# Moving the modulation dots of a decoder block's output stage, and the order of channels in its first two w_out tiles

## The chip, the core and the metric

The kernel runs on one core of one Trainium2 chip. The metric is the device time of one execution in microseconds (us). The engines are TensorE (PE; PEld is its loading of stationary weights), VectorE (DVE), ScalarE (ACT), GpSimd (POOL) and SyncE (SP), which here only issues transfers between HBM and the on-chip memory.

## The reference

One decoder block over 512 tokens and 1024 channels, in fp32. Cut to what matters:

```python
mod = c @ w_ada + b_ada                      # 6 x 1024 numbers
sh_a, sc_a, gt_a, sh_m, sc_m, gt_m = split(mod, 6)
h = modulate(rmsnorm(x, g_mix), sh_a, sc_a)
z = h @ w_in                                 # q, k, v, latents and two gates zga, zgb
o_nsa = nsa_attention(...)                   # 8 heads
o_mla = mla_attention(...)                   # 8 heads
y = sigmoid(zga) * (o_nsa @ w_o_nsa) + sigmoid(zgb) * (o_mla @ w_o_mla)
x = x + gt_a * (y @ w_out)
h = modulate(rmsnorm(x, g_mlp), sh_m, sc_m)
x = x + gt_m * (square(relu(h @ w_fc1)) @ w_fc2)
return rmsnorm(x, g_final)
```

The modulation `c @ w_ada` is 48 columns of 128 results. sh_a and sc_a are wanted first; gt_a, sh_m, sc_m and gt_m (the late ones) only behind the attention.

## The kernel before, in words

Channels lie on the 128 partitions, the 512 tokens on the free axis. 1024 channels are 8 tiles. Every product of an fp32 weight with an fp32 activation is made of three matmuls of rounded (fp32r) parts: each is split into a high part (a copy on ACT, L183 for weights, L192 for activations) and a low part (a subtraction on DVE, L184 and L193), and `mm3` (L197, L198, L199) multiplies high by high, high by low and low by high. A unit of weights is 128x1024 fp32, 512 KB. `wsplit` loads it on SP's queue into one of **four** `w_raw` buffers (L175) and splits it into w_hi and w_lo (three buffers each); with `far` the parts are called wp_hi and wp_lo and lie in another pool.

A modulation dot (`ada_dot`, L105 and L107) is not a matmul. It loads a 128x1024 piece of w_ada, also 512 KB, on SP's queue into one of the same four w_raw buffers, and DVE multiplies it by c and sums over the free axis into one column of `mod`. `ada_late(u)` makes two dots and adds the bias (L118); `ada_fill(end)` calls it for the next units up to `end`. Units 8 to 23 are the late ones, 32 dots in all.

The stages around the change, with their times in the profiled execution:

- MLA heads (about 232 to 328 us). The order is a string by hand, `ORDER`: `p` prepares the V products (vm), `a` makes q and k of a pair of heads, `b` their scores and softmax, `m` their values, `g1` one of the sixteen late gates (`gate_unit`: 24 matmuls with a w_z unit, then a tanh into tab), and `e1` one unit of the late modulation. `e1` stands there twice (units 8 and 9).
- Late gates (about 328 to 380): `fill(16)` makes what is left of the sixteen gates, and `ada_fill(12)` units 10 and 11.
- Output projections (about 380 to 421): for each of 8 tiles n, o_nsa by one half of w_o into the accumulator ps_acc and o_mla by the other half into ps_s. DVE multiplies each by its gate (ya, L759; yb, L761), POOL adds them into yb (L762), ACT and DVE split the sum into y*n*h and y*n*l. Behind each tile `ada_fill(12 + n + 1)` asks for one unit (12 to 19).
- w_out (from about 421): four whole tiles and then four in halves of the tokens, each a sum over all eight y tiles, 24 matmuls with 512 columns for a whole tile. Units 20 to 23 are asked for behind them. Then the MLP.

Nearly all of this is one stream for a scheduler. It writes a static order of instructions for each engine, in the order of the code as far as data and buffers allow, with the splits of weights ahead of others (`high_priority`). On the chip each engine, and SP's queue of transfers, then runs its list strictly in that order. A transfer into a w_raw buffer is issued once the last reader of that buffer is done. PSUM has two buffers for ps_acc and two for ps_s.

Of the kernel before, what the change touches and what calls it, by code (L numbers as in the profile page):

```python
# [13 lines left out]
ALU = mybir.AluOpType  # L14
PSUM = bass.MemoryType.PSUM

P = 128
S = 512
D = 1024
KT = D // P  # L20
# [19 lines left out]
FAR = 2  # L40
EV = "v"
NA = ["1"]
ORDER = "f0 t0 s0 t1 f1 h v0 c s1 v1 s2 g1 v2 g1 q w0 s3 w2 v3 w1 k g1 p g1 g1 a1 w3 a0 b1 a2 e1 b0 a3 m1 b3 e1 m3 m0 g1 b2 m2"


@with_exitstack
def block_kernel(ctx: ExitStack, tc: tile.TileContext, d):
    nc = tc.nc
# [3 lines left out]
    def psum(tag):  # L52
        bufs = PB[tag]
        return ps.tile([P, S], F32, name="ps_" + tag, tag=tag, bufs=bufs)
# [11 lines left out]
    def tmp(name):  # L66
        return sb.tile([P, S], F32, name=name, tag="tmp", bufs=NB["tmp"])

    def f(ap):
        return ap.bitcast(F32)  # L70


    def wtile(shape=(P, 1024)):
        return sb.tile(list(shape), F32, name="w_raw", tag="w_raw", bufs=NB["raw"])
# [97 lines left out]
    def wsplit(src, shape, far=False):  # L172
        n = int(np.prod(shape))
        raw = wtile()
        nc.sync.dma_start(raw[:, :n], src)  # L175
        if far:
            hi = sb.tile([P, 1280], F32R, name="wp_hi", tag="p", bufs=NB["p"])
            lo = sb.tile([P, 1280], F32R, name="wp_lo", tag="p", bufs=NB["p"])
        else:
            hi = sb.tile([P, 1024], F32R, name="w_hi", tag="w_hi", bufs=NB["hi"])  # L180
            lo = sb.tile([P, 1024], F32R, name="w_lo", tag="w_lo", bufs=NB["lo"])
        with tc.high_priority():
            nc.scalar.activation(hi[:, :n], raw[:, :n], AF.Copy)  # L183
            nc.vector.tensor_tensor(lo[:, :n], raw[:, :n], f(hi[:, :n]), op=ALU.subtract)  # L184
        pat = "p (a b) -> p a b" if len(shape) == 2 else "p (a b c) -> p a b c"
        kw = dict(zip("abc", shape))
        return hi[:, :n].rearrange(pat, **kw), lo[:, :n].rearrange(pat, **kw)

    def split(name, src, get):
        hi = get(name + "h", F32R)  # L190
        lo = get(name + "l", F32R)
        nc.scalar.activation(hi, src, AF.Copy)  # L192
        nc.vector.tensor_tensor(lo, src, f(hi), op=ALU.subtract)  # L193
        return hi, lo

    def mm3(out, w, x, first, last):
        nc.tensor.matmul(out, w[0], x[0], start=first, stop=False)  # L197
        nc.tensor.matmul(out, w[0], x[1], start=False, stop=False)  # L198
        nc.tensor.matmul(out, w[1], x[0], start=False, stop=last)  # L199

    def dense(out, unit, rhs, tok=ALL):
        hi, lo = unit
        n = len(rhs)
        for k in range(n):
            mm3(out[:, tok], (hi[:, k], lo[:, k]), (rhs[k][0][:, tok], rhs[k][1][:, tok]), k == 0, k == n - 1)
# [25 lines left out]
    h = []  # L231
# [192 lines left out]
    w2 = w2_th[:, 0:256].rearrange("p (k n c) -> p k n c", k=2, n=2)  # L424
# [240 lines left out]
    def gate_unit(i):  # L665
        pz = z_unit(9 + i)
        t = big_n(f"tab{i}")
        nc.scalar.activation(t, pz, AF.Tanh, scale=0.5)
        tab[i] = t
# [3 lines left out]
    def ada_late(u):  # L673
        for r in range(2):
            ada_dot(2 * u + r)
        bias_col(2 * u, 2)
# [5 lines left out]
    gi = [0]  # L682

    def fill(n):
        for _ in range(n):
            if gi[0] < 16:
                gate_unit(gi[0])
                gi[0] += 1

    ai = [8]  # L690

    def ada_fill(end):

        while ai[0] < min(end, 24):
            ada_late(ai[0])
            ai[0] += 1

    mqk, msc, lat = {}, {}, {}
    for step in ORDER.split():
        op, a = step[0], int(step[1:] or 0)  # L700
# [27 lines left out]
            fill(a)  # L728
        elif op == "e":
            ada_fill(ai[0] + a)  # L730
    fill(16)
    ada_fill(12)


    oh = []
# [15 lines left out]
    y = []  # L751
    for n in range(KT):
        w = wsplit(d["w_o"][n], (KT, P))
        pa = psum("acc")
        dense(pa, (w[0][:, 0:4], w[1][:, 0:4]), o_sp[0:4])
        pb = psum("s")
        dense(pb, (w[0][:, 4:8], w[1][:, 4:8]), o_sp[4:8])
        ta = tmp("ya")
        nc.vector.scalar_tensor_tensor(ta, tab[n], 1.0, pa, op0=ALU.add, op1=ALU.mult)  # L759
        tb = tmp("yb")  # L760
        nc.vector.scalar_tensor_tensor(tb, tab[8 + n], 1.0, pb, op0=ALU.add, op1=ALU.mult)  # L761
        nc.gpsimd.tensor_tensor(tb, ta, tb, op=ALU.add)  # L762
        y.append(split(f"y{n}", tb, big_a))
        ada_fill(12 + n + 1)
    st1 = Stats(KT, -1)

    def out_tile(n, pa, tok):
        nc.vector.scalar_tensor_tensor(xt[n][:, tok], pa[:, tok], modb[:, GTA + n:GTA + n + 1], xt[n][:, tok],
                                       op0=ALU.mult, op1=ALU.add)
        st1.add(xt[n], tok=tok)  # L770

    for n in range(KT - NH1):
        w = wsplit(d["w_out"][n], (KT, P))
        pa = psum("acc")
        dense(pa, w, y)
        out_tile(n, pa, ALL)

    for k in range(KT):
# [2 lines left out]
    ws = [wsplit(d["w_out"][n], (KT, P), n < KT - 2) for n in range(KT - NH1, KT)]  # L781
    for hf, tok in enumerate(HALVES):
        for n, w in zip(range(KT - NH1, KT), ws):
            pa = psum("acc")
# [170 lines left out]
    for qq in range(4):  # L955
# [3 lines left out]
        if qq == 0:  # L959
            ws = [wsplit(d["w_fc1"][UNITS[n]], (KT, P), n < FAR) for n in range(NPRE)]  # L960
# [6 lines left out]
        for i, n in enumerate(UNITS):  # L967
# [3 lines left out]
            if i in pre:  # L971
                pa = pre[i]
            else:
                w = wsplit(d["w_fc1"][8 * qq + n], (KT, P))
                pa = psum(("acc", "acc", "m", "o")[i % 4])
# [4 lines left out]
        if qq < 3:  # L980
            for i in range(2):
                w = wsplit(d["w_fc1"][8 * qq + 8 + UNITS[i]], (KT, P))
                pa = psum("acc")
# [14 lines left out]
    ws = [wsplit(d["w_fc2"][3, n], (KT, P), n < KT - 2) for n in range(nf, KT)]  # L998
    for hf, tok in enumerate(HALVES):
        for n, w in zip(range(nf, KT), ws):  # L1000
            pa = psum("s")
# [5 lines left out]
        k = 0  # L1007
# [120 lines left out]
```

## Time and profile before

| | us |
|---|---|
| median of three runs | 830.43 (828.70 to 832.08) |
| the profiled execution, its own time | 831.55 |
| its span, from the first to the last record | 829.8 |
| PE busy in the span | 798.3 (96%) |
| DVE busy | 606.2 (73%) |
| ACT busy | 392.1 (47%) |
| POOL busy | 148.0 (18%) |

The profile is of one execution. An engine's busy time counts its instructions, without the waits; a busy PE may still run at the lower of its two clocks, 1.2 instead of 2.4 GHz, which the granted clock (PEclk, as a share of full speed) shows. A wait in the trace is the idle time ahead of an instruction, put down to the one that released it last. Since each engine runs in a fixed order, an idle PE means that the next matmul on its list lacks an operand or a place to write to; whether that costs time is seen from the starts of the matmuls around it.

### The profile page before, as it was taken

Reading aid. Unit: us, or ns where it says so; the run is one execution under the profiler, and the core shown is the slowest. Engines: PE = TensorE matmul, PEld = TensorE weight load, DVE = VectorE, ACT = ScalarE, POOL = GpSimd, SP = SyncE. Lnnn points to the kernel's source line nnn. Section 1 sums busy time; section 2 is a strip of 40 time slices with the busy share of each in tenths; the row PEclk is TensorE's granted clock in tenths of the full one; section 3 lists DMA queues with packets and bytes.
Section 4 is the critical chain, followed back from the end, with each engine's and each line's share of the span. In section 5 each row is a group of like instructions: output and inputs, shape, how many; then the busy total and the mean of one; then the engine's idle time right before and its main releaser. Section 6 shows DMA issues by size and latency. Waiting matters only on the chain.

```text
span 829.8 us, 11895 instructions
## 1 busy us (share of the span) xinstructions
PE 798.3 (96%) x4444; PEld 646.3 (78%) x4444; DVE 606.2 (73%) x1177; ACT 392.1 (47%) x742; POOL 148.0 (18%) x125
## 2 busy tenths in 40 slices
PE   5899999999999999999989999999999999999896
PEld 3687668665577665888768998899889988998895
DVE  5988758887657886367877648887668766877854
ACT  4358526475333443222232437644564456445741
POOL 1500000000000000002330003460336033613200
PEclk8999999999999999999999999999999999999998
DMA  9683161010032122587647302233323332332303
GB/s 336 233 275 139 56 224 51 27 51 26 26 128 76 52 77 69 170 260 255 228 159 254 110 18 85 94 103 127 101 77 103 127 102 76 103 128 77 102 1 102
DMA packets 31004, 99.76 MB, mean 120 GB/s; under 512 B 3521, under 2 KB 5761, under 8 KB 30946
## 3 DMA queue, kind: packets, MB, share of 16 engines
q1 hardware_dynamic: 30880, 98.89, 36.0%
q8 instruction: 35, 0.57, 0.3%
q14 instruction: 23, 0.19, 0.1%
q0 software_dynamic: 64, 0.11, 0.1%
q10 hardware_dynamic: 2, 0.00, 0.0%
HBM read 96.89 MB, written 2.10 MB: 119 GB/s over the span
## 4 chain that ended last, share of the span: by engine, by line
PE 74%; DVE 11%; DMA 5%; ACT 3%; POOL 3%; issue 3%; SPq 0%; DVEq 0%; POOLq 0%; ACTq 0%
PE ps_acc L197 10%; PE ps_acc L199 10%; PE ps_acc L198 10%; PE ps_s L858 8%; PE ps_t L858 6%; PE ps_t L391 4%; DVE junk L107 3%; PE ps_o L572 3%; DMA w_raw<-in_w_ada_dram 3%; PE ps_s L644 2%; PE ps_o L657 2%; PE ps_s L197 1%; PE ps_s L198 1%; PE ps_s L199 1%; POOL yb L762 1%
## 5 line engine op out<-in xcount | busy, mean ns | idle before, releaser
L184 DVE TENSOR_TENSOR w_lo<-w_raw,w_hi 128x1024 fp32r<-128x1024 f32 x76 | 96.1, 1266 | 62.8 <-ACT w_hi L183 62.4
L183 ACT ACTIVATE w_hi<-w_raw 128x1024 fp32r<-128x1024 f32 x76 | 80.2, 1058 | 125.5 <-PE ps_acc L198 68.8
L346 ACT ACTIVATE p<-p,nm 128x128 f32<-128x128 f32 (+3 forms) x96 | 53.3, 556 | 58.1 <-DVE nm L344 56.8
L198 PE MATMUL ps_acc<-hl,w_hi 128*128 128x512 f32 x200 | 80.1, 400 | 0.0
L199 PE MATMUL ps_acc<-hh,w_lo 128*128 128x512 f32 x200 | 80.0, 400 | 0.0
L197 PE MATMUL ps_acc<-hh,w_hi 128*128 128x512 f32 x200 | 79.3, 397 | 0.0
L379 DVE COPY pT<-ps_t 128x512 f32<-128x512 f32 (+1 forms) x72 | 42.4, 598 | 31.1 <-PE ps_o L572 16.6
L816 ACT ACTIVATE ws_hi<-wsum 128x512 fp32r<-128x512 f32 x56 | 35.3, 631 | 58.0 <-POOL wsum L829 55.3
L107 DVE SCALAR_TENSOR_TENSOR junk<-w_raw,cb 128x1024 bf16<-128x1024 f32 x32 | 40.0, 1255 | 16.8 <-DMA w_raw<-in_w_ada_dram 16.7
L829 POOL TENSOR_TENSOR wsum<-w_raw 128x512 f32<-128x512 f32 x28 | 39.5, 1410 | 64.9 <-DMA w_raw<-in_w_fc_dram 53.4
L829 POOL TENSOR_TENSOR wsum<-wsum,w_raw 128x512 f32<-128x512 f32 x28 | 45.9, 1640 | 25.6 <-DVE ws_lo L817 25.2
L817 DVE TENSOR_TENSOR ws_lo<-wsum,ws_hi 128x512 fp32r<-128x512 f32 x56 | 42.9, 796 | 4.9 <-ACT ws_hi L816 2.5
L198 PEld LDWEIGHTS ps_acc<-hl,w_hi 128*128 128x128 f32 x200 | 37.6, 188 | 11.0 <-issue 4.3
L199 PEld LDWEIGHTS ps_acc<-hh,w_lo 128*128 128x128 f32 x200 | 37.6, 188 | 10.0 <-issue 3.1
L197 PEld LDWEIGHTS ps_acc<-hh,w_hi 128*128 128x128 f32 x200 | 37.6, 188 | 9.8 <-issue 3.0
L197 PE MATMUL ps_acc<-h2h,w_hi 128*128 128x512 f32 x112 | 43.6, 389 | 0.0
L198 PE MATMUL ps_acc<-h2l,w_hi 128*128 128x512 f32 x112 | 43.6, 389 | 0.0
L199 PE MATMUL ps_acc<-h2h,w_lo 128*128 128x512 f32 x112 | 43.6, 389 | 0.0
L762 POOL TENSOR_TENSOR yb<-ya,yb 128x512 f32<-128x512 f32 x8 | 17.5, 2185 | 133.3 <-DVE yb L761 123.2
L858 PE MATMUL ps_t<-t,ws_hi 128*128 128x256 f32 x224 | 40.5, 281 | 0.7 <-DVE t L946 0.4
L391 PEld LDWEIGHTS ps_t<-ident,p 128*128 128x128 f32 x240 | 27.7, 141 | 16.3 <-issue 6.3
L817 DVE TENSOR_TENSOR w_lo<-w_raw,w_hi 128x1024 fp32r<-128x1024 f32 (+1 forms) x28 | 31.0, 1107 | 10.2 <-ACT w_hi L816 10.2
(478 smaller groups left out, 2305.1 us busy)
## 6 DMA issues: line engine op xcount, KB each, us to landing
w_raw<-in_w_fc_dram SPq DMA_DIRECT2D x64, 512.0 KB, 3.3
w_raw<-in_w_ada_dram SPq DMA_DIRECT2D x32, 512.0 KB, 3.9
w_raw<-in_w_z_dram SPq DMA_DIRECT2D x25, 512.0 KB, 3.6
w_ada<-in_w_ada_dram SPq DMA_DIRECT2D x16, 512.0 KB, 6.6
w_raw<-in_w_c_dram SPq DMA_DIRECT2D x8, 512.0 KB, 4.5
w_raw<-in_w_o_dram SPq DMA_DIRECT2D x8, 512.0 KB, 4.4
w_raw<-in_w_out_dram SPq DMA_DIRECT2D x8, 512.0 KB, 3.3
w_raw<-in_w_g_dram SPq DMA_DIRECT2D x8, 448.0 KB, 7.2
```

Of the source, the lines that this page charges most:

```text
L107: nc.vector.scalar_tensor_tensor(junk, w, 1.0, cb, op0=ALU.mult, op1=ALU.mult, accum_out=mod[:, col:col + 1])
L183: nc.scalar.activation(hi[:, :n], raw[:, :n], AF.Copy)
L184: nc.vector.tensor_tensor(lo[:, :n], raw[:, :n], f(hi[:, :n]), op=ALU.subtract)
L197: nc.tensor.matmul(out, w[0], x[0], start=first, stop=False)
L198: nc.tensor.matmul(out, w[0], x[1], start=False, stop=False)
L199: nc.tensor.matmul(out, w[1], x[0], start=False, stop=last)
L346: nc.scalar.activation(o, o, AF.Exp, bias=nm, scale=-1.0, accum_out=sm)
L379: nc.vector.tensor_copy(dst, src)
L391: nc.tensor.transpose(pp[:, off:off + P], aps[i][:, kb * P:(kb + 1) * P], ident)
L817: nc.vector.tensor_tensor(lo, src, f(hi), op=ALU.subtract)
L829: nc.gpsimd.tensor_tensor(t, sums[x_] if isinstance(x_, int) else x_, y_, op=ALU.add)
L858: nc.tensor.matmul(out, w[a_][:, k], x[k][b_], start=(first and k == 0 and j == 0), stop=(k == 3 and j == 2), skip_group_check=True)
```

## The change

The sixteen late units are asked for at other places, one of the adds changes its engine, and two tiles of w_out are made together.

- `ORDER` has `e1` four times: units 8 to 11 are made in the MLA heads, one ahead of two gates near `p`, two at the old places, one ahead of the last pair's scores.
- Behind every second late gate one unit is asked for (12 to 17). Units 18 and 19 follow the projections of tiles 1 and 3; behind the other projections there is none. Units 20 to 23 stay.
- For the projections of tiles 6 and 7 the sum of ya and yb is made on DVE, for the other six still on POOL.
- The first two w_out tiles are summed side by side, the first in ps_acc and the second in ps_s: channels 0 to 5 of the first, 0 to 5 of the second, then 6 and 7 of the first and 6 and 7 of the second.

```diff
-ORDER = "... k g1 p g1 g1 a1 w3 a0 b1 a2 e1 b0 a3 m1 b3 e1 m3 m0 g1 b2 m2"
+ORDER = "... k g1 p e1 g1 g1 a1 w3 a0 b1 a2 e1 b0 a3 m1 b3 e1 m3 m0 g1 e1 b2 m2"
...
-    fill(16)
-    ada_fill(12)
+    while gi[0] < 16:
+        fill(1)
+        if gi[0] % 2 == 0:
+            ada_fill(min(ai[0] + 1, 18))
+    ada_fill(18)
...
-        nc.gpsimd.tensor_tensor(tb, ta, tb, op=ALU.add)
+        (nc.vector if n >= KT - 2 else nc.gpsimd).tensor_tensor(tb, ta, tb, op=ALU.add)
         y.append(split(f"y{n}", tb, big_a))
-        ada_fill(12 + n + 1)
+        if n in (1, 3):
+            ada_fill(ai[0] + 1)
...
+    NL = 2
+    ws = [wsplit(d["w_out"][n], (KT, P)) for n in range(2)]
+    pas = [psum("acc"), psum("s")]
+    for ks in (range(KT - NL), range(KT - NL, KT)):
+        for w, pa in zip(ws, pas):
+            for k in ks:
+                mm3(pa, (w[0][:, k], w[1][:, k]), y[k], k == 0, k == KT - 1)
     for n in range(KT - NH1):
-        w = wsplit(d["w_out"][n], (KT, P))
-        pa = psum("acc")
-        dense(pa, w, y)
+        if n < 2:
+            pa = pas[n]
+        else:
+            w = wsplit(d["w_out"][n], (KT, P))
+            pa = psum("acc")
+            dense(pa, w, y)
         out_tile(n, pa, ALL)
```

On SP's queue, from the V products to the late gates, the order before was this (w_uv holds the V weights, w_uqk the q and k weights, w_z the gates' weights, w_ada the dots'; the first two w_z loads here are those of gates 3 and 4, the next ones of gate 5 on):

```order
L175 DMA w_raw<-in_w_uv_dram 128x1024
L175 DMA w_raw<-in_w_z_dram 128x1024 x2
L175 DMA w_raw<-in_w_uqk_dram 128x1024 x3
L105 DMA w_raw<-in_w_ada_dram 128x1024 x2
L175 DMA w_raw<-in_w_uqk_dram 128x1024
L105 DMA w_raw<-in_w_ada_dram 128x1024 x2
L175 DMA w_raw<-in_w_z_dram 128x1024 x8
```

With the change it is this:

```order
L175 DMA w_raw<-in_w_uv_dram 128x1024
L105 DMA w_raw<-in_w_ada_dram 128x1024 x2
L175 DMA w_raw<-in_w_z_dram 128x1024 x2
L175 DMA w_raw<-in_w_uqk_dram 128x1024 x3
L105 DMA w_raw<-in_w_ada_dram 128x1024 x2
L175 DMA w_raw<-in_w_uqk_dram 128x1024
L105 DMA w_raw<-in_w_ada_dram 128x1024 x2
L175 DMA w_raw<-in_w_z_dram 128x1024
L105 DMA w_raw<-in_w_ada_dram 128x1024 x2
L175 DMA w_raw<-in_w_z_dram 128x1024 x2
L105 DMA w_raw<-in_w_ada_dram 128x1024 x2
```

The loads of pairs of dots now stand ahead of those of the gates, and between them: behind the load of gate 5 two of dots, then gates 6 and 7, two of dots, gates 8 and 9. On DVE in the MLA heads, at the end of the third pair's scores (L344 and L369 are of the softmax, L379 copies transposed p for PE, L360 is the softmax's reciprocal), the order before was:

```order
L107 SCALAR_TENSOR_TENSOR junk,mod<-w_raw,cb 128x1024
L360 RECIPROCAL rc<-sm 128x4
L107 SCALAR_TENSOR_TENSOR junk,mod<-w_raw,cb 128x1024
L369 TENSOR_SCALAR p<-p,rc 128x128
L369 TENSOR_SCALAR p<-p,rc 128x384
L369 TENSOR_SCALAR p<-p,rc 128x512
L118 TENSOR_TENSOR modb<-mod,cols 128x2
L379 COPY pT<-ps_t 128x512 x2
L184 TENSOR_TENSOR w_lo<-w_raw,w_hi 128x1024
L379 COPY pT<-ps_t 128x256
L379 COPY pT<-ps_t 128x512
```

With the change:

```order
L107 SCALAR_TENSOR_TENSOR junk,mod<-w_raw,cb 128x1024
L360 RECIPROCAL rc<-sm 128x4
L107 SCALAR_TENSOR_TENSOR junk,mod<-w_raw,cb 128x1024
L369 TENSOR_SCALAR p<-p,rc 128x128
L369 TENSOR_SCALAR p<-p,rc 128x384
L369 TENSOR_SCALAR p<-p,rc 128x512
L118 TENSOR_TENSOR modb<-mod,cols 128x2
L379 COPY pT<-ps_t 128x512 x2
L379 COPY pT<-ps_t 128x256
L184 TENSOR_TENSOR w_lo<-w_raw,w_hi 128x1024
L379 COPY pT<-ps_t 128x512
L184 TENSOR_TENSOR w_lo<-w_raw,w_hi 128x1024
```

Two splits of gate weights stand among the copies now, in place of one. On DVE in the projections, around tile 4 (one tile of the eight), the order before was:

```order
L193 TENSOR_TENSOR y3l<-yb,y3h 128x512
L107 SCALAR_TENSOR_TENSOR junk,mod<-w_raw,cb 128x1024
L759 SCALAR_TENSOR_TENSOR ya<-tab_2172,ps_acc 128x512
L107 SCALAR_TENSOR_TENSOR junk,mod<-w_raw,cb 128x1024
L761 SCALAR_TENSOR_TENSOR yb<-tab_3018,ps_s 128x512
L118 TENSOR_TENSOR modb<-mod,cols 128x2
L184 TENSOR_TENSOR w_lo<-w_raw,w_hi 128x1024
L114 SCALAR_TENSOR_TENSOR amlp<-mod,badd,cols 128x1
L193 TENSOR_TENSOR y4l<-yb,y4h 128x512
```

With the change (ya and yb stand on lines 763 and 765 there):

```order
L193 TENSOR_TENSOR y3l<-yb,y3h 128x512
L763 SCALAR_TENSOR_TENSOR ya<-tab_2181,ps_acc 128x512
L765 SCALAR_TENSOR_TENSOR yb<-tab_3063,ps_s 128x512
L184 TENSOR_TENSOR w_lo<-w_raw,w_hi 128x1024
L193 TENSOR_TENSOR y4l<-yb,y4h 128x512
```

The dots and their sums of columns are gone from between the products. On PE in the first w_out tile the order before was:

```order
L199 MATMUL ps_acc<-y5h,w_lo 128x512
L197 MATMUL ps_acc<-y6h,w_hi 128x512
L198 MATMUL ps_acc<-y6l,w_hi 128x512
L199 MATMUL ps_acc<-y6h,w_lo 128x512
L197 MATMUL ps_acc<-y7h,w_hi 128x512
L198 MATMUL ps_acc<-y7l,w_hi 128x512
L199 MATMUL ps_acc<-y7h,w_lo 128x512
L197 MATMUL ps_acc<-y0h,w_hi 128x512
```

With the change, from the last product of y5 with the second tile on:

```order
L199 MATMUL ps_s<-y5h,w_lo 128x512
L197 MATMUL ps_acc<-y6h,w_hi 128x512
L198 MATMUL ps_acc<-y6l,w_hi 128x512
L199 MATMUL ps_acc<-y6h,w_lo 128x512
L197 MATMUL ps_acc<-y7h,w_hi 128x512
L198 MATMUL ps_acc<-y7l,w_hi 128x512
L199 MATMUL ps_acc<-y7h,w_lo 128x512
L197 MATMUL ps_s<-y6h,w_hi 128x512
```

The products with y6 and y7 stand behind 36 others now, where y6 stood behind 18 and y7 behind 21.

## Rows read from the trace of the kernel before

**Rows 1.** The page: busy time, share of the span and instructions of each engine.

```profile
PE 798.3 (96%) x4444; PEld 646.3 (78%) x4444; DVE 606.2 (73%) x1177; ACT 392.1 (47%) x742; POOL 148.0 (18%) x125
```

**Rows 2.** Table by stage: stretch, length, engines' busy us (instructions), PEclk, DMA share, GB/s.

```profile
core 0: us, PE busy (x) PEld busy (x) DVE busy (x) ACT busy (x) POOL busy (x), PEclk, DMA share, GB/s
232.00:281.00 49.00, 48.95 (x208) 36.87 (x207) 34.89 (x81) 19.38 (x45) 2.45 (x4) 1.00 0.30 97
281.00:328.00 47.00, 46.64 (x224) 26.71 (x223) 36.22 (x90) 19.39 (x49) 0.00 (x0) 1.00 0.18 55
328.00:380.00 52.00, 52.00 (x230) 42.99 (x229) 26.78 (x43) 14.42 (x19) 0.00 (x0) 1.00 0.70 229
380.00:421.00 41.00, 39.74 (x171) 31.74 (x170) 32.91 (x55) 11.46 (x14) 13.48 (x7) 1.00 0.66 212
421.00:433.00 12.00, 8.45 (x30) 6.37 (x29) 10.68 (x11) 5.25 (x7) 4.00 (x2) 0.86 0.53 175
```

**Rows 3.** PE's waits: engine, operation, line, released by: us, times, longest.

```profile
PE ps_acc L197 <- ACT y7h L192: 3.0, 1, 3.0
...
PE ps_acc L197 <- DVE ya L759: 1.0, 1, 1.0
```

**Rows 4.** Timeline of PE, projections: start, us, line, operation [idle before <- releaser].

```profile
407.71 0.39 PE L199 MATMUL ps_s<-ohl,w_lo 128*128 128x512 f32 x1
409.08 0.47 PE L197 MATMUL ps_acc<-ohl,w_hi 128*128 128x512 f32 x1 [0.97 <-DVE ya L759]
...
414.48 0.40 PE L199 MATMUL ps_s<-ohl,w_lo 128*128 128x512 f32 x1
415.17 0.47 PE L197 MATMUL ps_acc<-ohl,w_hi 128*128 128x512 f32 x1 [0.29 <-DVE amlp L114]
```

**Rows 5.** Timeline of DVE, projections: one modulation dot.

```profile
407.10 1.22 DVE L107 SCALAR_TENSOR_TENSOR junk<-w_raw,cb 128x1024 bf16<-128x1024 f32 x1
```

**Rows 6.** Timeline of PE, first w_out tile.

```profile
420.79 0.39 PE L197 MATMUL ps_acc<-y0h,w_hi 128*128 128x512 f32 x1
...
425.35 0.39 PE L199 MATMUL ps_acc<-y6h,w_lo 128*128 128x512 f32 x1
428.76 0.51 PE L197 MATMUL ps_acc<-y7h,w_hi 128*128 128x512 f32 x1 [3.03 <-ACT y7h L192]
429.79 0.80 PE L198 MATMUL ps_acc<-y7l,w_hi 128*128 128x512 f32 x1 [0.52 <-DVE y7l L193]
...
432.89 0.39 PE L199 MATMUL ps_acc<-y1h,w_lo 128*128 128x512 f32 x1
```

**Rows 7.** Timeline of DVE and POOL, first w_out tile.

```profile
423.92 0.68 DVE L193 TENSOR_TENSOR y6l<-yb,y6h 128x512 fp32r<-128x512 f32 x1
425.12 0.67 DVE L761 SCALAR_TENSOR_TENSOR yb<-tab,ps_s 128x512 f32<-128x512 f32 x1
425.96 2.09 POOL L762 TENSOR_TENSOR yb<-ya,yb 128x512 f32<-128x512 f32 x1 [3.05 <-DVE yb L761]
426.85 2.28 DVE L184 TENSOR_TENSOR wp_lo<-w_raw,wp_hi 128x1024 fp32r<-128x1024 f32 x1
```

**Rows 8.** Timeline of DVE and PE at the V products in the MLA heads.

```profile
232.62 0.69 DVE L525 TENSOR_TENSOR o<-o,ps_m 128x512 f32<-128x512 f32 x1 [0.31 <-PE ps_m L523]
234.21 0.69 DVE L379 COPY vm<-ps_acc 128x512 f32<-128x512 f32 x1 [0.90 <-PE ps_acc L199]
235.37 0.39 PE L197 MATMUL ps_acc<-w_hi,ckv0h 128*128 128x512 f32 x1
```

**Rows 9.** Timeline of DVE and ACT, third pair of MLA heads.

```profile
294.56 1.20 DVE L107 SCALAR_TENSOR_TENSOR junk<-w_raw,cb 128x1024 bf16<-128x1024 f32 x1
296.81 1.06 ACT L183 ACTIVATE w_hi<-w_raw 128x1024 fp32r<-128x1024 f32 x1 [1.61 <-PE ps_acc L198]
297.90 1.23 DVE L184 TENSOR_TENSOR w_lo<-w_raw,w_hi 128x1024 fp32r<-128x1024 f32 x1
```

**Rows 10.** The page's DMA issues (KB each, us to landing), then a wait of DVE.

```profile
w_raw<-in_w_z_dram SPq DMA_DIRECT2D x25, 512.0 KB, 3.6
w_ada<-in_w_ada_dram SPq DMA_DIRECT2D x16, 512.0 KB, 6.6
...
DVE junk L107 <- DMA w_raw<-in_w_ada_dram: 16.7, 11, 3.6
```

More of the change, by code (lines that the diff above doesn't have):

```diff
@@ L42 @@
 NA = ["1"]
-ORDER = "f0 t0 s0 t1 f1 h v0 c s1 v1 s2 g1 v2 g1 q w0 s3 w2 v3 w1 k g1 p g1 g1 a1 w3 a0 b1 a2 e1 b0 a3 m1 b3 e1 m3 m0 g1 b2 m2"
+ORDER = "f0 t0 s0 t1 f1 h v0 c s1 v1 s2 g1 v2 g1 q w0 s3 w2 v3 w1 k g1 p e1 g1 g1 a1 w3 a0 b1 a2 e1 b0 a3 m1 b3 e1 m3 m0 g1 e1 b2 m2"
 @with_exitstack
```

## The prediction

> **What bounds the kernel now.** The page comes first: PE is busy for 798.3 us, 96% of the span [rows 1]. The matmuls of both kernels are the same, so time can only come out of stretches in which PE stands still or runs at a lower clock, and it can only be lost by making new ones. The table by stage shows where such stretches lie in the part that the change touches [rows 2]. The MLA heads (232 to 328) leave PE idle for 0.05 and 0.36 us, the late gates (328 to 380) for nothing; there 230 matmuls take 52.00 us, 0.226 us each, and I take 0.23 as the step from one matmul to the next. The output projections (380 to 421) lose 1.26 us, and the first w_out tile (421 to 433) 3.55 us, at a granted clock of 0.86 where every other stretch has 1.00. The list of PE's waits names the causes there: y7h with 3.0 us, ya with 1.0 [rows 3].
>
> **What the change takes away.** Two losses, each measured from start to start, less the normal steps.
>
> First, the projections. The matmul at 407.71 is followed by one at 409.08, 1.37 us later in place of 0.23, and the one at 414.48 by one at 415.17, 0.69 us later [rows 4]. The first waits for ya, which must empty the accumulator; on DVE a modulation dot of 1.22 us, begun at 407.10, stands just before ya [rows 5]. Together 1.14 + 0.46 = 1.6 us. In the changed order no dot stands on DVE between the first ya and the last, and the column products (amlp) that stood there too are done in the gates. I take all 1.6 us as gained.
>
> Second, y7. The last y6 matmul starts at 425.35, the first y7 one at 428.76, the next at 429.79, and the normal step is back at 432.89 [rows 6]. That is nine steps in 7.54 us; nine normal ones are 2.07, so 5.47 us are lost. The first two steps are 3.18 and 0.80 us too long; the other 1.49 us go to the lower of the two clocks, 1.2 GHz, which PE was granted right after standing still (the 0.86 of that stretch). Without the standing still I expect no fall of the clock: with the stop of 0.97 us at 409.08 in it, the stretch of the projections was granted 1.00 [rows 2, 4].
>
> Is y7 in time now? The chain is yb (425.12, 0.67 us), the add on POOL (2.09), y7h on ACT, y7l on DVE [rows 7]. w_out starts at 420.79 [rows 6]. Before, PE asks for y7h after 21 matmuls; now after 39, at 420.79 + 39 x 0.23 = 429.8, and for y7l at 430.0. Suppose DVE is as late as before: yb ends at 425.8, the add on DVE takes as long as yb (0.68, my estimate from the yb row, the same size), so y7h can start at 426.5 and is ready near 427.2. Behind the add stand w_lo and wp_lo; wp_lo took 2.28 us beside POOL's add, and 1.23 is what a subtraction of this size took without it [rows 9], so y7l ends near 426.5 + 1.23 + 1.23 + 0.68 = 429.6. That is 0.4 us before it is wanted, with DVE as late as it was; and it will be less late, because twelve of the sixteen dots that lay in the projections' code are gone from it. y6 is wanted at 429.1 and was split by 424.6. w_out[1] is now wanted after 18 matmuls instead of 24, 1.4 us sooner, and its split is on DVE before y6's. So the wait goes and nothing takes its place there. Gain so far: 1.6 + 5.5 = **7.1 us**.
>
> **What it adds and moves.** The dots keep their number and their price (1.22 us [rows 5] and a short read of the sum, about 1.3 together). They move to DVE's queue in the MLA heads and the gates, and their 512 KB loads on SP's queue go in front of the late gates' weights, in the same four w_raw buffers. In the gates PE needs one tile of weights in 5.5 us (24 x 0.23); DVE has 26.78 of 52 us busy, ACT 14.42 and the DMA engines 70% [rows 2], so two dots for every second gate are hidden there: cost nothing. If that cover were gone, the eight dots that come to the gates would cost up to 1.3 us each. Three transfers of x now stand on SP's queue before two gate loads, which are wanted some 10 us later: nothing.
>
> In the MLA heads DVE is the busy engine (34.89 of 49 and 36.22 of 47 us [rows 2]) and PE's next work often comes out of it, so moved work costs there. Three places:
> - The V products. Two dots, 2.6 us, now stand between the first and the second copy of vm. Before, DVE was idle for 0.90 us ahead of the second copy, at 234.21, and ahead of that it had added o (128x512 as the copy, so about 0.7), which now stands later [rows 8]. So the second copy comes 2.6 - 0.9 - 0.7 = 1.0 us later, at 235.2, and ends at 235.9. The fourth product, begun at 235.37, writes over that copy's buffer: 0.5 us late. I take 0.4, between 0 and the 1.3 of one dot.
> - Gate weights 6 and 7. Before, these were loaded long ahead. Now two dots of the next unit hold two of the four buffers, so each load is issued only when a dot has been done; in the old trace the second of two begins at 294.56 [rows 9] and is done at 295.8. A w_z load lands after 3.6 us [rows 10], ACT's split takes 1.06, so the second subtraction could start at about 295.8 + 3.6 + 1.06 = 300.5. DVE would reach it at 297.90 + 0.42 + 1.23 + 0.69 = 300.2 (the subtraction's old start, a short copy, one subtraction, a copy). DVE waits some 0.3 us, does one subtraction more than before (1.23), and the copies of the transposed p that PE wants stand behind it. PE has 18 gate matmuls in that place, 4.1 us, for cover. I take 0.7; from 0 (fully covered) to 3.7, if a load takes the 6.6 us that is the median of the w_ada loads at the start [rows 10].
> - Gate weights 8 and 9, the same with the last pair of heads: dots after om0's copy, the subtractions among the copies of the last pair. I take 0.8; 0 to 3.8.
>
> Below nothing: PE's order changes between the two kinds of matmul 17 times here instead of 19, worth at most 0.2 us. Sum of the additions **1.9 us**, from -0.2 to 8.8.
>
> All else is the same: behind the second w_out half the order is unchanged on every engine. Eight dots remain for the w_out tiles in both. Without the stop in front of y7, DVE has 5.5 us less for them, some four dots, and the six w_out tiles that follow take PE far longer than the eight (8 x 1.3 = 10.4 us): hidden, nothing.
>
> **Sum.** 7.1 - 1.9 = 5.2 us less. The profiled execution took 831.55 us (span 829.8 and 1.75 around it), so 826.3 on its scale; the median of the runs is 830.43, 1.1 us less than the profiled one, and against it the forecast is **825.2 us**.
>
> **The rivals.**
> - *The heads give most of it back.* Loads of 4 to 5 us in place of 3.6 at both places of gate weights, each held on DVE and passed on to PE, make the additions 3 to 7 us: 826.5 to 830.5, middle 828.4. For it: DVE's queue is in order, and the two loads of a pair overlap. Against: filler matmuls stand beside each. The Trainium skill has a rule that speaks for this rival: *DMA: Bandwidth & Descriptors*, section Rules for kernel authors, says to issue a DMA early, compute, and wait for it late, so that the fixed cost is hidden; the change does the opposite for four gate loads. No row here shows a late w_z load, since none was late. Chance 0.22.
> - *y7 is late all the same.* The margin above is 0.4 us if DVE is as late as before, and wp_lo waits for a w_out load. If w_out[5] lands 3 us late, y7l is late by 2.6: 827.8. For it: SP's queue sends the eight w_out loads one after the other, and DVE's order has wp_lo ahead of y6l and y7l. Against: these loads now follow w_o loads with few dots between. Chance 0.08.
> - *Slower.* The four buffers starve the heads: at gate weights 6, 7, 8 and 9 DVE stands still for a whole load of 3.6 us, because every load must wait for a dot, every dot for its own load, in one queue; PE's fillers (gates 5 to 7) need the very weights that are late and are no cover. 4 x 3.6 = 14.4 us in place of the 1.5 that I have: 825.2 + 12.9 = 838 us. It decides as soon as such waits take 5.2 us more than I have, since the gain is gone then. Against: in the old trace DVE waited 11 times for a w_ada load, 16.7 us in all and 3.6 at most [rows 10], and PE stood still for none of it. Chance 0.05.
> - *It does not do what it says*: the scheduler might have put the dots back. The order shows that it has not. Chance nil.
>
> **How the numbers follow.** Forecast, additions of 0 to 3 us: chance 0.65, 823.3 to 826.3. Faster by over 0.5% (about what a measurement of this kernel can tell from no change) means below 826.3: the forecast's 0.65 and a little of the first rival, 0.66. Within 0.5%, 826.3 to 834.6: most of the first rival and the second, 0.29. Slower: 0.05. The range takes in the forecast, the late y7 and most of the first rival: **822.3 to 829.6**, where the lower end also allows 1 us for the scatter of the runs.
>
> **What would show it.** In the changed profile: no wait of PE for y7h or y7l, and a clock of 1.00 between 400 and 440; no wait for ya over 0.3 us. The loss in the heads should show as PE idle time of 1 to 3 us between 232 and 330, with DVE's w_lo waiting for w_hi and that for a w_z load. PE idle of 5 us or more there, or a wait for y7l, would make the forecast wrong.

## The result, and the profile after

The changed kernel takes 822.03 us (median of 6 runs, 820.9 to 823.5); the kernel before took 830.59 us beside it (6 runs, 828.7 to 832.4). The ratio is 0.9896, with an interval of 0.9880 to 0.9912: 8.6 us less, of which 7.3 to 10.0 are sure. The forecast was 825.2 us, 5.2 us less, with a range down to 822.3. The time lies just below that range: the direction was right, the size was not. Medians and ratios are of undisturbed executions; one execution of the order string alone, below, took 1579.85 us and is left out.

The profiled execution of the changed kernel took 820.9 us, with a span of 819.1. Its page (the row of busy times, answering to [rows 1]):

```profile
PE 796.0 (97%) x4444; PEld 645.2 (79%) x4444; DVE 608.7 (74%) x1179; ACT 393.0 (48%) x742; POOL 141.1 (17%) x123
```

The table by stage of the changed kernel, with the columns of [rows 2]; the stretches are the same stages, moved to where they now lie:

```profile
229.40:278.40 49.00, 48.95 (x209) 36.64 (x207) 36.15 (x85) 17.96 (x43) 2.45 (x4) 1.00 0.33 108
278.40:325.00 46.60, 46.60 (x223) 27.12 (x221) 37.48 (x92) 20.62 (x48) 0.00 (x0) 1.00 0.27 85
325.00:377.00 52.00, 52.00 (x231) 42.53 (x231) 35.73 (x66) 15.29 (x20) 0.00 (x0) 1.00 0.83 279
377.00:416.00 39.00, 39.00 (x170) 31.70 (x170) 27.16 (x30) 12.69 (x15) 10.95 (x6) 1.00 0.36 121
416.00:427.00 11.00, 11.00 (x51) 9.06 (x50) 6.50 (x9) 3.89 (x5) 0.00 (x0) 1.00 0.49 150
```

PE is busy for the whole length of every stretch but the first, which lacks 0.05 us, and the clock is 1.00 in all five. The 1.26 us that the projections lost, the 3.55 us and the clock of 0.86 at the first w_out tile, and the 0.36 us in the second half of the heads are gone. No wait of PE for ya, y7h, y7l or pT is left in its list of waits.

To compare many executions I use one table from here on. It gives, from the starts of matmuls in each trace, the length of four stages: **heads** (first V product to first projection, so with the late gates), **projections** (to the first w_out matmul), **w_out** (to the MLP's first matmul into ps_s, three behind its very first) and **MLP** (to the end of the span), all in us. By this count the projections of the kernel before begin at 374.70 us, earlier than the rounded 380 of the list of stages.

| kernel | first V product at | heads | projections | w_out | MLP |
|---|---|---|---|---|---|
| before | 228.84 | 145.86 | 46.09 | 52.22 | 356.77 |
| after | 226.22 | 145.53 | 44.33 | 46.79 | 356.26 |
| gain | 2.62 | 0.33 | 1.76 | 5.43 | 0.51 |

The gains add up to 10.65 us, the difference of the two spans. The three stages that the change touches give **7.52 us**. The 2.62 us ahead of them belong to no edit: the list of work is the same there, and the eleven executions of other kernels below reach the first V product between 226.83 and 228.52 us, whatever their edits. That is the scatter of one execution, and medians are less open to it.

### The profile page after: what moved, and what is told of

The parts are those of the page before. It is cut to its first block, busy times and chain, and to the rows that moved or that the text cites. A ratio compares the mean times of both kernels' runs of the same rounds, so it can differ in the third digit from the quotient of the medians.

```text
span 819.1 us, 11898 instructions
## 1 busy us (share of the span) xinstructions
PE 796.0 (97%) x4444; PEld 645.2 (79%) x4444; DVE 608.7 (74%) x1179; ACT 393.0 (48%) x742; POOL 141.1 (17%) x123
## 4 chain that ended last, share of the span: by engine, by line
PE 83%; DVE 7%; ACT 3%; DMA 2%; issue 2%; POOL 2%; SPq 0%; DVEq 0%; POOLq 0%; ACTq 0%
PE ps_acc L197 12%; PE ps_acc L199 12%; PE ps_acc L198 12%; PE ps_s L874 8%; PE ps_t L874 6%; PE ps_t L391 4%; PE ps_o L572 4%; PE ps_s L197 3%; PE ps_s L198 3%; PE ps_s L199 3%; PE ps_s L644 2%; PE ps_o L657 2%; POOL wsum L845 2%; DMA w_raw<-in_w_fc_dram 1%; DVE junk L107 1%
## 5 line engine op out<-in xcount | busy, mean ns | idle before, releaser
L184 DVE TENSOR_TENSOR w_lo<-w_raw,w_hi 128x1024 fp32r<-128x1024 f32 x76 | 99.5, 1311 | 54.4 <-ACT w_hi L183 54.2
L379 DVE COPY pT<-ps_t 128x512 f32<-128x512 f32 (+1 forms) x72 | 42.4, 599 | 28.1 <-PE ps_o L572 15.8
L391 PE MATMUL ps_t<-ident,p 128*128 128x128 f32 x240 | 37.2, 279 | 0.0
```

The source lines that it names most:

```text
L379: nc.vector.tensor_copy(dst, src)
L391: nc.tensor.transpose(pp[:, off:off + P], aps[i][:, kb * P:(kb + 1) * P], ident)
```

## The experiments

All times are medians, with the kernel before run beside them on the same chip. The first four take the change apart. In the timeline rows of DVE the short read of the sum behind each dot is left out without a mark.

**The order string alone.** Four units in the heads, everything else as before.

```diff
-ORDER = "... k g1 p g1 g1 a1 ... m0 g1 b2 m2"
+ORDER = "... k g1 p e1 g1 g1 a1 ... m0 g1 e1 b2 m2"
```

> The kernel before with the changed order string alone: units 10 and 11 of the modulation are made in the MLA heads too, the rest as before (units 12 to 19 stay behind the projections, the w_out tiles and the adds are as before). Theory A (what moves into the heads is covered there, and the one wait of PE for pT of 0.36 us goes): 0 to 0.5 us less than before, no wait of PE between 230 and 330 us over 0.3 us. Theory B (the heads do cost what was forecast, 1.9 us, and the time that the whole change gained beyond the forecast comes from elsewhere): 1.5 to 2.3 us more than before, with PE idle between 230 and 330 us.

Measured: 831.56 us against 830.83, ratio 1.0010 (0.9995 to 1.0024). No gain, and no sure loss. The stages tell more: heads 145.65, 0.2 less than before, but projections 48.64, 2.55 more. So the heads bear the moved dots for nothing, as theory A had it, and the loss lies where neither theory looked. The list of PE's waits, and the start of DVE's timeline in the projections:

```profile
PE ps_acc L197 <- DVE ya L759: 3.3, 4, 1.6
...
385.06 1.23 DVE L107 SCALAR_TENSOR_TENSOR junk<-w_raw,cb 128x1024 bf16<-128x1024 f32 x1 [3.21 <-DMA w_raw<-in_w_ada_dram]
```

A dot stands on DVE ahead of y0 low, waits 3.21 us for its own load, and makes DVE late for the tiles that follow; ya is then waited for four times instead of once.

**The dots alone**, in the heads, the gates and behind projections 1 and 3, as in the change; the w_out tiles one by one and all adds on POOL (shown against the changed kernel).

```diff
-        (nc.vector if n >= KT - 2 else nc.gpsimd).tensor_tensor(tb, ta, tb, op=ALU.add)
+        nc.gpsimd.tensor_tensor(tb, ta, tb, op=ALU.add)
...
-    ws = [wsplit(d["w_out"][n], (KT, P)) for n in range(2)]
...
+    for n in range(KT - NH1):
+        w = wsplit(d["w_out"][n], (KT, P))
+        pa = psum("acc")
+        dense(pa, w, y)
```

> The change without its two other edits: the dots are moved as in the change, all eight adds stay on POOL, and the w_out tiles are made one by one. Theory A (the three edits overlap: with the dots gone from the projections DVE is 4 to 5 us less late at y7, so the wait for y7 goes by this alone): y7h is ready about 1 us ahead of its matmul, y7l at its matmul or up to 0.5 us late; 6.5 to 7.5 us less than before. Theory B (the edits add up, and y7 needs the interleaved w_out tiles): the gain is the 1.6 us of the projections and less than half of the 5.5 of y7, 1.6 to 4 us less.

Measured: 821.66 us against 830.83, ratio 0.9897 (0.9880 to 0.9915): all that the whole change gained. Heads 145.46, projections 44.33, w_out 47.06. DVE and PE at y7 in this kernel:

```profile
416.93 0.69 DVE L765 SCALAR_TENSOR_TENSOR yb<-tab,ps_s 128x512 f32<-128x512 f32 x1
418.94 2.32 DVE L184 TENSOR_TENSOR wp_lo<-w_raw,wp_hi 128x1024 fp32r<-128x1024 f32 x1
421.18 0.68 DVE L193 TENSOR_TENSOR y7l<-yb,y7h 128x512 fp32r<-128x512 f32 x1
...
421.52 0.39 PE L197 MATMUL ps_acc<-y7h,w_hi 128*128 128x512 f32 x1
421.91 0.50 PE L198 MATMUL ps_acc<-y7l,w_hi 128*128 128x512 f32 x1
422.25 0.40 PE L199 MATMUL ps_acc<-y7h,w_lo 128*128 128x512 f32 x1
```

yb starts 0.19 us after the first w_out matmul (416.74), where before it started 4.33 us after it [rows 6, 7]. With DVE on time, POOL's slow add and w_out in the old order cost PE some 0.3 us: the steps to and behind the y7l matmul are 0.39 and 0.34 in place of 0.23. Theory A holds; the gain, 8.6 us by the ratio and at least 7.1, is above its 6.5 to 7.5 by the median.

**The interleaved w_out tiles alone**, dots and adds as before.

```diff
+    for ks in (range(KT - NL), range(KT - NL, KT)):
+        for w, pa in zip(ws, pas):
+            for k in ks:
+                mm3(pa, (w[0][:, k], w[1][:, k]), y[k], k == 0, k == KT - 1)
```

> The kernel before with the first two w_out tiles interleaved alone; dots and adds as before. Theory A: y7h, ready at 428.7 us before, is now wanted 39 matmuls behind the start of w_out, at 429.8, so the wait of 5.5 us goes even with the dots and POOL's add in place, and ya still waits in the projections; 5 to 5.8 us less than before. Theory B (edits add up): y7l is late by 1 us or more, or w_out[1], wanted 1.4 us sooner, is; 2 to 4.5 us less.

Measured: 828.34 us against 830.83, ratio 0.9976 (0.9963 to 0.9988): 2.0 us less by the ratio. Theory A was right that y7 isn't waited for and wrong on the gain; the gain lies in theory B's range, but neither of B's causes is there. PE's waits and DVE's timeline, with a timeline row of PE between:

```profile
PE ps_acc L197 <- DVE xr L768: 1.9, 1, 1.9
...
445.46 0.39 PE L197 MATMUL ps_acc<-y0h,wp_hi 128*128 128x256 f32 x1 [1.92 <-DVE xr L768]
...
442.37 1.22 DVE L107 SCALAR_TENSOR_TENSOR junk<-w_raw,cb 128x1024 bf16<-128x1024 f32 x1
443.51 1.22 DVE L107 SCALAR_TENSOR_TENSOR junk<-w_raw,cb 128x1024 bf16<-128x1024 f32 x1
444.66 0.74 DVE L768 SCALAR_TENSOR_TENSOR xr<-ps_acc,modb,xr 128x512 f32<-128x512 f32 x1
```

PE no longer stops for y7 at 428, but 17 us later, for an accumulator that DVE empties behind two dots. The lateness went on to the next place where PE needs DVE.

**The two adds on DVE alone.**

```diff
-        nc.gpsimd.tensor_tensor(tb, ta, tb, op=ALU.add)
+        (nc.vector if n >= KT - 2 else nc.gpsimd).tensor_tensor(tb, ta, tb, op=ALU.add)
```

> The kernel before with the adds of tiles 6 and 7 on DVE alone. Theory A and B: y7h is ready at about 427.2 us in place of 428.7 and y7l at 428.4 in place of 429.8, still 1.6 and 2.2 us after PE wants them; PE stands still for about 2.5 us, and the clock may fall again; 2 to 3 us less than before. What tells: whether the fall of the clock to 1.2 GHz (1.5 us) comes behind a stop of 1.6 us too.

Measured: 830.44 us against 830.83, ratio 0.9997 (0.9986 to 1.0007): nothing, where 2 to 3 us were expected. PE's waits:

```profile
PE ps_acc L197 <- ACT y7h L192: 1.7, 1, 1.7
PE ps_acc L197 <- DVE ya L759: 1.6, 1, 1.6
PE ps_acc L198 <- DVE y7l L193: 1.1, 1, 1.1
```

The wait for y7h fell from 3.0 to 1.7, that for y7l rose from 0.5 to 1.1, and that for ya from 1.0 to 1.6. By the stages, w_out gained 0.7 us and the projections lost 0.9. The expectation also asked whether the clock falls behind a shorter stop. It did behind these two stops in a row: the granted clock was 0.53 in the mean from 428 to 431 us, and the steps between matmuls were 0.43 in place of 0.23:

```profile
428.54 0.63 PE L199 MATMUL ps_acc<-y7h,w_lo 128*128 128x512 f32 x1
428.96 0.63 PE L197 MATMUL ps_acc<-y0h,w_hi 128*128 128x512 f32 x1
```

**Both w_out edits, with the dots left in the projections:** the case that the forecast's sum supposed ("with DVE as late as before").

```diff
-        nc.gpsimd.tensor_tensor(tb, ta, tb, op=ALU.add)
+        (nc.vector if n >= KT - 2 else nc.gpsimd).tensor_tensor(tb, ta, tb, op=ALU.add)
...
+            for k in ks:
+                mm3(pa, (w[0][:, k], w[1][:, k]), y[k], k == 0, k == KT - 1)
```

> The kernel before with both edits at w_out (two tiles interleaved, the adds of tiles 6 and 7 on DVE) and the dots left in the projections. This is the case that the forecast supposed, with DVE as late as before. Theory A (DVE's lag isn't removed, it is only met later, at xr of the third w_out tile, where PE stood still for 1.9 us in the run with the interleaved tiles alone; without POOL beside it wp_lo is 1 us shorter): y7 not waited for, the stop at xr 0.5 to 1.5 us; 3 to 4 us less than before. Theory B (the forecast's sum): 5 to 5.8 us less, no stop behind y7.

Measured: 827.96 us against 830.69, ratio 0.9969 (0.9956 to 0.9982), 2.6 us less. y7 isn't waited for, and the stop at xr is larger than with the tiles alone, not smaller:

```profile
PE ps_acc L197 <- DVE xr L768: 2.4, 1, 2.4
```

w_out gained 2.7 us by the stages where the change gained 5.43, and the stop at xr is 2.4 of the difference. So the interleaving by itself doesn't bring the 5.5 us. Theory A had the mechanism, but not the size.

**All eight adds on DVE**, the dots left in the projections. If the stops at ya and at y7 are one lag, a shorter round on DVE should remove both. The round of one tile before, from DVE's timeline of the kernel before:

```profile
385.36 0.69 DVE L193 TENSOR_TENSOR y0l<-yb,y0h 128x512 fp32r<-128x512 f32 x1 [1.84 <-ACT y0h L192]
385.97 1.22 DVE L107 SCALAR_TENSOR_TENSOR junk<-w_raw,cb 128x1024 bf16<-128x1024 f32 x1
387.11 0.68 DVE L759 SCALAR_TENSOR_TENSOR ya<-tab,ps_acc 128x512 f32<-128x512 f32 x1
387.71 1.22 DVE L107 SCALAR_TENSOR_TENSOR junk<-w_raw,cb 128x1024 bf16<-128x1024 f32 x1
388.86 0.68 DVE L761 SCALAR_TENSOR_TENSOR yb<-tab,ps_s 128x512 f32<-128x512 f32 x1
...
389.66 1.22 DVE L184 TENSOR_TENSOR w_lo<-w_raw,w_hi 128x1024 fp32r<-128x1024 f32 x1
392.73 0.69 DVE L193 TENSOR_TENSOR y1l<-yb,y1h 128x512 fp32r<-128x512 f32 x1 [1.86 <-ACT y1h L192]
```

From y0l to y1l DVE takes 7.37 us, 1.86 of them idle until POOL's add and ACT's copy are done; PE needs 24 x 0.23 = 5.5 us for a tile. In such a round, with two dots, DVE falls 1.9 us behind. From y0l to y7l there are seven rounds: three with two dots (7.37, 7.56 and 7.24 us), one with one dot (6.20) and three without (5.01 to 5.18), 43.7 us in all where PE needs 38.8 (seven eighths of 44.33 us, what the projections take PE with the change). So the lag is built up in the first four and only partly made good in the last three. In the round of 7.56 us the idle time is missing, but the second dot takes 2.32 us beside POOL's add.

```diff
-        nc.gpsimd.tensor_tensor(tb, ta, tb, op=ALU.add)
+        nc.vector.tensor_tensor(tb, ta, tb, op=ALU.add)
```

> The kernel before with all eight adds of the projections on DVE, nothing else; the dots stay in the projections. Theory A (the waits for ya and for y7 are one lag: with two dots in a tile DVE's round yb, POOL's add, the split on ACT, y low, dot, ya, dot takes some 7.4 us where PE needs 5.4, so DVE falls behind tile by tile, and y7 is late by what is left of that): with the add on DVE the round is yb 0.6, add 0.6, w_lo 1.1 beside ACT's split, y low 0.6, dot 1.1, ya 0.6, dot 1.1, some 5.8 us, the lag all but goes, no wait for ya over 0.5 us, y7 late by 1 us at most; 5 to 7 us less than before. Theory B (the dots alone make DVE late, the adds on POOL are off the path): at most 1 us less than before, as the two adds alone gave, or slower, since DVE has 4 us more work.

Measured: 823.29 us against 831.77, ratio 0.9908 (0.9884 to 0.9932). Projections 44.33, w_out 47.20, no wait for ya or y7h, and 0.2 us for y7l. Two steps of its round on DVE:

```profile
391.33 0.69 DVE L193 TENSOR_TENSOR y1l<-yb,y1h 128x512 fp32r<-128x512 f32 x1
...
397.34 0.69 DVE L193 TENSOR_TENSOR y2l<-yb,y2h 128x512 fp32r<-128x512 f32 x1
```

The round, with two dots in it too, is 6.01 us where it was 7.37, though it has 0.6 us more work. Theory A holds; the median gain of 8.5 us is above its 5 to 7, though the interval, 5.7 to 9.6, overlaps it. DVE had time for the work; what it had not was time to wait for POOL.

**The dots out of the projections, but none into the heads.**

```diff
-ORDER = "... k g1 p e1 g1 g1 a1 ... m0 g1 e1 b2 m2"
+ORDER = "... k g1 p g1 g1 a1 ... m0 g1 b2 m2"
```

(against the changed kernel; w_out and the adds as in the run of the dots alone)

> The dots leave the projections, as in the change, but none goes to the MLA heads: the order string is that of before, one unit behind every second late gate, the rest of units up to 17 behind the last gate; w_out tiles one by one, adds on POOL. Theory A (what counts is that no dot stands on DVE among the projections; the heads neither cost nor give): 0 to 1.5 us more than the run with dots moved and nothing else, 7 to 9 us less than before. Theory B (the gates have no room for 18 dots without the heads): PE waits in the gates or at ya again, 3 us or more above that run.

Measured: 822.51 us against 831.77, ratio 0.9903 (0.9880 to 0.9927); heads 145.59, projections 44.33, w_out 47.04. Theory A holds: the dots of units 10 to 17 fit beside the gates without a stop, and the four new dots in the heads were not needed.

**More dots in the heads.** The forecast charged the four new dots there with 1.9 us. Three runs raise the dose: 12, 16 and 24 dots (8 in the changed kernel).

```diff
-ORDER = "... k g1 p e1 g1 g1 a1 w3 a0 b1 a2 e1 b0 a3 m1 b3 e1 m3 m0 g1 e1 b2 m2"
+ORDER = "... k g1 p e2 g1 g1 a1 w3 a0 b1 a2 e2 b0 a3 m1 b3 e2 m3 m0 g1 e2 b2 m2"
```

(12 dots: e2 at the first and third place alone; 24 dots: e3 at all four)

> The changed kernel with two units at the first and the third place of the MLA heads (behind the V products, and behind the third pair's scores) and one at the others: 12 dots in the heads, between the changed kernel's 8, which cost nothing, and 16, which cost 16 us. Theory A (each place bears one unit, since two of the four buffers are left for weights; a second unit takes all four): the stops of the 16-dot run at these two places come back, 2.3 us at km and 4.7 at w_hi and what follows from them, 5 to 10 us over the changed kernel. Theory B (the total is what counts, with some slack left at 8): 0 to 4 us.

> The changed kernel with two units at each of the four places in the MLA heads (16 dots there instead of 8), fewer in the gates. DVE was busy for 73.6 of 95.6 us there with 8 dots; 8 more at 1.2 us make 83. Theory A (a moved instruction costs nothing as long as DVE's list has idle time ahead of what PE wants, and PE's gates beside the heads cover the rest): 0 to 2 us more than the changed kernel. Theory B (the forecast's view, each pair of dots delays gate weights and transposed p): 0.5 us for each dot, some 4 us more, with PE waiting for pT or w_lo.

> As the run before, with three units at each place: all 24 dots of units 8 to 19 in the MLA heads, none in gates or projections. DVE would be busy for 93 of 95.6 us. Theory A: the cover is used up, PE stands still behind DVE; 3 to 10 us more than the changed kernel. Theory B: 0.5 us for each of 16 dots more, 8 us. The two part at the run before; this one tells how far the cover reaches.

| dots in the heads | median, us | ratio to before | heads, us |
|---|---|---|---|
| 8 (after) | 822.03 | 0.9896 (0.9880 to 0.9912) | 145.53 |
| 12 | 832.12 | 1.0020 (1.0008 to 1.0031) | 155.17 |
| 16 | 838.33 | 1.0091 (1.0064 to 1.0117) | 160.37 |
| 24 | 847.75 | 1.0200 (1.0173 to 1.0227) | 169.99 |

Both theories for 16 dots were wrong: not 0 to 2 nor 4 us over the changed kernel, but 16. So were both for 24: not 3 to 10 nor 8, but 26. The run with 12 lost 10.1 us, the upper end of its theory A, but only one of that theory's two stops came back: behind the V products, where the second unit stands first, PE was busy for 56.63 of the first 56.75 us and no km was waited for. The loss came from the third place. The largest stop there, and what stands before it on ACT and SP (timeline):

```profile
244.69 10.94 SPq L105 DMA_DIRECT2D w_raw<-in_w_ada_dram  x4
292.88 0.33 SPq L175 DMA_DIRECT2D w_raw<-in_w_z_dram  x1
...
296.18 1.06 ACT L183 ACTIVATE w_hi<-w_raw 128x1024 fp32r<-128x1024 f32 x1 [2.69 <-DMA w_raw<-in_w_z_dram]
297.29 0.79 PE L197 MATMUL ps_acc<-hh,w_hi 128*128 128x512 f32 x1 [4.83 <-ACT w_hi L183]
```

and SP in the changed kernel:

```profile
247.35 0.33 SPq L175 DMA_DIRECT2D w_raw<-in_w_z_dram  x1
253.23 6.27 SPq L105 DMA_DIRECT2D w_raw<-in_w_ada_dram  x2
290.95 1.54 SPq L175 DMA_DIRECT2D w_raw<-in_w_z_dram  x2
```

With 12 dots four loads of w_ada in a row take all four buffers at 245 to 255 us. The dots, which stand behind the third pair's scores, give them back one by one, the first at 292.76 us and the last at 297.25. The gate's weight is loaded into the first of them at 292.88, and the next matmul on PE's list needs it: PE stands still for 4.83 us, and then was granted a clock of 0.50, the lower of its two levels, from 297.2 to 302.0 us. In the whole of the heads PE's idle time was 5.8 us of the 9.6 that they lost; most of the rest goes with the lower clock (0.92 in the mean from 285 to 330 us). In the changed kernel a gate's weights were loaded at 247.35, ahead of the two dots, and PE spent the stretch from 287.94 to 294.04 mostly on that gate, while the next two loads, issued at 290.95, came in.

**Is it the buffers or DVE's time?** The kernel with 16 dots, where the second unit of each place reads the resident c and loads nothing.

```diff
-            w = wtile()
-        nc.sync.dma_start(w, d["w_ada"][col])
+            w = wtile() if load else cb
+        if load:
+            nc.sync.dma_start(w, d["w_ada"][col])
...
-            ada_dot(2 * u + r)
+            ada_dot(2 * u + r, load=u not in (9, 11, 13, 15))
```

> The run with two units at each place of the MLA heads, but the second unit of each place (units 9, 11, 13, 15) makes its two dots from the resident c in place of a piece of w_ada: the eight loads and their turns in the four w_raw buffers are left out, the dots' time on DVE stays. Theory A (the heads cost what they cost by the four buffers: a gate's weights wait for a dot, the dot for its own load): the 16 us that this kernel lost against the changed one go, 0 to 2.5 us over the changed kernel. Theory B (DVE's time is what runs out): the loss stays, 12 us or more over the changed kernel.

Measured: 824.80 us against 830.69, ratio 0.9933 (0.9917 to 0.9950); heads 147.25. Of the 16.3 us between 16 dots and 8, 13.5 go with the loads; 2.8 stay. The stretch from 282 to 340 us with loads, then without (columns of [rows 2]):

```profile
282.00:340.00 58.00, 49.77 (x221) 26.69 (x221) 43.64 (x105) 21.12 (x49) 0.00 (x0) 0.94 0.34 113
...
282.00:340.00 58.00, 56.75 (x265) 35.27 (x264) 48.93 (x114) 23.25 (x49) 0.00 (x0) 1.00 0.32 100
```

Without the loads DVE is busier (48.93 against 43.64 us) and PE idle for 1.25 us instead of 8.23. So it is the loads with their turns in the buffers above all, not DVE's time. This run takes away loads, buffers and queue time together and doesn't part them; the DMA engines were busy for 0.34 of this stretch with the loads and 0.32 without, so a lack of transfer rate is unlikely. The 2.8 us are a little over theory A's 2.5; 1.7 of them lie in the heads.

## Why the prediction was wrong, step by step

- **The projections, 1.6 us: right.** They gained 1.76, and no wait for ya is left.
- **y7, 5.5 us: right in size, wrong in reason.** w_out gained 5.43 us. The step "is y7 in time now?" rested it on the 39 matmuls and the adds on DVE, with DVE as late as before; that twelve dots leave the projections was named only as a reason for a wider margin. The run with just these two edits gained 2.6 us of the 8.6 and stood still at xr, a stop that the forecast didn't see; the run with the dots alone gained everything. The forecast had two causes where there is one: DVE's round of 7.4 us against PE's 5.5, through POOL's add and two dots, whose lag showed first at ya and then at y7. In the changed kernel y7l is done at 420.56, 4.6 us before PE asks for it at 425.17, where the forecast saw a margin of 0.4 us:

```profile
416.27 0.69 DVE L765 SCALAR_TENSOR_TENSOR yb<-tab,ps_s 128x512 f32<-128x512 f32 x1 [0.65 <-PE ps_s L199]
419.88 0.68 DVE L193 TENSOR_TENSOR y7l<-yb,y7h 128x512 fp32r<-128x512 f32 x1
...
425.17 0.39 PE L198 MATMUL ps_acc<-y7l,w_hi 128*128 128x512 f32 x1
```

- **The sentence that w_out's remaining dots are hidden: right here by luck.** In the changed kernel no xr is waited for. With the dots left in the projections, the same eight dots and the lag made a stop of 1.9 to 2.4 us there.
- **The additions in the heads, 1.9 us: this term failed.** The heads gained 0.33 us, and PE was idle for 0.05 us between 229.4 and 325 where the forecast named 1 to 3 us as the sign of this cost. Its first place, the V products: the forecast had the second copy of vm 1.0 us later and the fourth product 0.5 us late.

```profile
229.61 1.21 DVE L107 SCALAR_TENSOR_TENSOR junk<-w_raw,cb 128x1024 bf16<-128x1024 f32 x1
230.75 1.22 DVE L107 SCALAR_TENSOR_TENSOR junk<-w_raw,cb 128x1024 bf16<-128x1024 f32 x1
231.90 0.68 DVE L379 COPY vm<-ps_acc 128x512 f32<-128x512 f32 x1
...
232.75 0.40 PE L197 MATMUL ps_acc<-w_hi,ckv0h 128*128 128x512 f32 x1
```

The copy ends at 232.58, 0.17 us before the product. Start to start the two dots take 2.29 us, not 2.6, and the 0.31 us of idle time ahead of o, which stands in [rows 8], had been left out: the copy came 0.31 us later (231.90 + 2.62 against 234.21), not 1.0. The second place, gate weights 6 and 7: the forecast had the second subtraction at 300.5, which is 297.9 on the new scale, and DVE waiting some 0.3 us.

```profile
297.94 1.23 DVE L184 TENSOR_TENSOR w_lo<-w_raw,w_hi 128x1024 fp32r<-128x1024 f32 x1 [0.77 <-ACT w_hi L183]
```

The start was met within 0.1 us. What was wrong is the step from there to PE, "I take 0.7": PE had the matmuls of a gate to do and lost nothing. At gates 8 and 9 it was the same, with a wait of 0.51 us on DVE and none on PE. The forecast had named this cover and charged for it all the same. And a stop of 0.36 us for pT in the heads of before was not in the sum; it is gone.
- **The sum.** 7.1 less 1.9 was forecast; 7.19 plus 0.33 is what the two traces show. With the heads at nothing the forecast would have been 823.3 us. The last 1.1 us to the measured 8.6 can't be put to a place: they are less than the interval's half width of 1.3 us. The range's lower end took the heads' least price of nothing at 823.3 and 1 us for scatter, too little when several terms come out at their good end. (The first rival's bounds are 0.2 us off its own sum: additions of 3 to 7 us give 826.3 to 830.3, not 826.5 to 830.5.)
- **The rivals.** "The heads give it back" and "slower" have a real mechanism, four buffers and one queue, but one unit at a place cost nothing, and a second did at the third place: with 12 dots the time was 832.1 us, slower than before. The Trainium skill, *DMA: Bandwidth & Descriptors*, section Rules for kernel authors, says to issue a DMA early, compute, and wait for it late. The traces agree where the issue is really late, as with the load at 292.88, whose matmul waited 4.83 us, and show no cost where other weights were loaded first.

## What to carry to other kernels

Stops of the bottleneck engine that follow one another in a loop may be one lag: compare the round of the engine that feeds it (here 7.4 us) with its own (5.5 us) before putting a price on each. Curing the last stop alone (interleaved tiles) moves the lag on to the next buffer; shortening the round, by taking either the dots or another engine's slow add out of it, removed them here but for 0.2 to 0.3 us. Work moved under another stage was free here as long as its buffers left the next operand of the bottleneck loaded ahead, and the price jumped (0, 10, 16 and 26 us for 8, 12, 16 and 24 dots) once they did not. Busy shares didn't show that: from 282 to 340 us DVE was busy for 75% with the loads and for 84% without them, and it was the first of the two that lost time.

## What the runs showed of the hardware

A DVE operation on 128x1024 fp32 with two operands in on-chip memory took 1.22 us alone and 2.28 to 2.35 us when POOL's add had begun before it (wp_lo at 418.94 above, and in [rows 7]). Where DVE began first, it was POOL's add that grew. Both orders stand in the changed kernel:

```profile
383.87 1.29 POOL L766 TENSOR_TENSOR yb<-ya,yb 128x512 f32<-128x512 f32 x1 [3.13 <-ACT w_hi L183]
383.89 2.34 DVE L184 TENSOR_TENSOR w_lo<-w_raw,w_hi 128x1024 fp32r<-128x1024 f32 x1 [0.17 <-ACT w_hi L183]
...
400.51 1.22 DVE L184 TENSOR_TENSOR w_lo<-w_raw,w_hi 128x1024 fp32r<-128x1024 f32 x1 [0.17 <-ACT w_hi L183]
400.57 2.32 POOL L766 TENSOR_TENSOR yb<-ya,yb 128x512 f32<-128x512 f32 x1 [4.34 <-ACT w_hi L183]
```

The later one ends 1.1 to 1.2 us after the end of the first. The Trainium skill, *SBUF — State Buffer*, section "SBUF: two separate sides", says that DVE (with two operands in SBUF) and GpSimd share one pair of ports as an exclusive lock, so that one waits for the other's whole instruction. These rows agree with it, as far as the profile's times of POOL, which are rough, can show. It changes how the round of the kernel before is read: its add on POOL took 2.35 us because w_lo, on DVE at 389.66, began 0.02 us before it, so by the same reading part of the 1.86 us for which DVE then waited came from its own split. With all adds on DVE every w_lo and wp_lo of the projections took 1.22 or 1.23 us.

PE's clock fell behind some stops and not behind others. The granted clock was 1.00 in the projections before, with a stop of 0.97 us [rows 2, 4], and 1.00 behind the stop of 1.92 us at xr with the tiles alone (445.46 to 452.00 us). It was 0.60 behind the 3.03 us at y7 (428.70 to 433.00), which is the 0.86 of the longer stretch, and 0.94 in the stretch of the run with 16 dots in which PE stood still for 8.23 us in all.
